# Linear attention on one core: the store of group 9 moved from GpSimd's software queue to SyncE's hardware queue

## The chip, the cores and the metric

One core of one Trainium2 chip. The metric is device time in microseconds (us) of one execution, median of several runs. Some programs have a second, slower state of execution. The profiled span (first to last instruction) is some 1.8 us shorter than the run time of the same execution.

## The reference

```python
# Q, K, V: 8 x 12 x 512 x 64, fp32
Q_feat = np.maximum(0, Q) + 1
K_feat = np.maximum(0, K) + 1
KV = np.einsum('bhkd,bhkv->bhdv', K_feat, V)
K_sum = np.sum(K_feat, axis=2)
numerator = np.einsum('bhqd,bhdv->bhqv', Q_feat, KV)
denominator = np.einsum('bhqd,bhd->bhq', Q_feat, K_sum)
return numerator / (denominator[:, :, :, None] + 1e-10)
```

Three inputs of 12.6 MB are read and one output of 12.6 MB is written: 50.3 MB of HBM traffic.

## The kernel before

The work is cut into 12 groups (NG = 12), each with 1 MB of output. K, V and Q are loaded through GpSimd, and these loads cast from fp32 to bf16 on the way (only the first K comes through SyncE, uncast). Each group's output is stored when its two halves have been normalised on VectorE.

```python
def store(g):
    s = g // 2
    o_to = o_dram[:, 2 * NP * s : 2 * NP * s + 2 * NP]
    if g < NG - 2:                                   # groups 0 to 9: GpSimd
        nc.gpsimd.dma_start(out=o_to[:, g % 2 : 2 * NP : 2], in_=outs[s][:, g % 2 : 2 * NP : 2])
        return
    if g == NG - 2:                                  # group 10: SyncE
        nc.sync.dma_start(out=o_to[:, 0 : 2 * NP : 2], in_=outs[s][:, 0 : 2 * NP : 2])
        return
    for h in range(2):                               # group 11: SyncE, in two halves
        nc.sync.dma_start(
            out=o_to[:, 2 * h + g % 2 : 2 * NP : NP], in_=outs[s][:, 2 * h + g % 2 : 2 * NP : NP]
        )

# ... the loop over groups 0 to 9: loads, compute, store(g - 3); the rest of the compute; store(7) ...
output(last - 1)                # last = 11
output(last)
for g in range(last - LAG, NG): # stores of groups 8, 9, 10, 11
    store(g)
```

(The comments are added here and passages cut, marked by "...". In the traces GpSimd and SyncE each issue their stores in the order of the program, each store after its data: group 9's at 110.19 us, 0.3 us after VectorE's last multiply for it.)

Of the kernel before, what the change touches and what calls it, by code (L numbers as in the profile page):

```python
# [19 lines left out]
def kernel(  # L20
# [19 lines left out]
    nc = tc.nc  # L40
# [8 lines left out]
    NP = 4  # L49
    NG = NPAIR // NP  # L50
# [37 lines left out]
    outs = {}  # L88
# [33 lines left out]
    def store(g):  # L122
        s = g // 2
        o_to = o_dram[:, 2 * NP * s : 2 * NP * s + 2 * NP]
        if g < NG - 2:
            nc.gpsimd.dma_start(out=o_to[:, g % 2 : 2 * NP : 2], in_=outs[s][:, g % 2 : 2 * NP : 2])  # L126
            return
        if g == NG - 2:
            nc.sync.dma_start(out=o_to[:, 0 : 2 * NP : 2], in_=outs[s][:, 0 : 2 * NP : 2])
            return  # L130
        for h in range(2):
            nc.sync.dma_start(
                out=o_to[:, 2 * h + g % 2 : 2 * NP : NP], in_=outs[s][:, 2 * h + g % 2 : 2 * NP : NP]
            )
# [112 lines left out]
    with tc.manual_schedule():  # L247
# [17 lines left out]
        for g in range(last - 1):  # L265
            if g % 2:
                transposes(g - 1)
            k_features(g)
            v_blocks(g)
            if g >= 2:  # L270
                output(g - 2)
            if g % 2:
                transposes(g)
            else:
                q_features(g)
                q_features(g + 1)
            keys_values(g)
            if g % 2 and g // 2 + 2 < NG // 2:
                load_pair(g // 2 + 2)
            if g >= LAG:  # L280
                store(g - LAG)
# [5 lines left out]
        v_blocks(last)  # L287
        keys_values(last - 1)
        store(last - 1 - LAG)
        q_features(last - 1)  # L290
        q_features(last)
# [8 lines left out]
        for g in range(last - LAG, NG):  # L300
            store(g)
# [30 lines left out]
```

## Time and profile before

| | before |
|---|---|
| median time, 3 runs | 126.77 us |
| profiled span | 125.0 us |
| busiest compute engine, VectorE | 89.1 us, 71% |
| DMA engines, share of software queue + hardware queue | 97.2% + 6.7% |

The profile's slice rows cut the span into 40 equal slices of 3.1 us; a digit is the busy share in tenths, and the GB/s row is what the 16 DMA engines moved. The prediction below shows these rows and the tail's timeline. A store has landed when its transfer is complete; the page's "us to landing" is the time from the start of the issuing instruction to the last of the 16 semaphore increments of the transfer.

### The profile page before, as it was taken

What the parts mean: (1) busy time and instruction counts of PE and PEld (TensorE: products, weight loads), DVE (VectorE), ACT (ScalarE), POOL (GpSimd) and SP (SyncE); (2) the same over time, 40 slices, a digit from 0 to 9 for tenths busy, and PEclk for the clock granted to TensorE, in tenths of its full rate; (3) what the DMA queues carried; (4) which work ended last, traced back from release to release, by engine and by line L of the source; (5) the groups of instructions that cost most, each with busy time, mean ns of one, the idle gap of its engine ahead of it and who ended that gap; (6) DMA issues with size and microseconds to landing.
All of it is one profiled execution on the core that took longest, in us unless ns stands there. A gap on an engine that the chain in (4) does not pass through costs nothing.

```text
span 125.0 us, 2348 instructions
## 1 busy us (share of the span) xinstructions
PE 62.7 (50%) x960; PEld 51.3 (41%) x960; DVE 89.1 (71%) x190; ACT 59.6 (48%) x86; POOL 26.1 (21%) x52
## 2 busy tenths in 40 slices
PE   0004945200593837539684691079494457775300
PEld 0003735200482827428573491057393255663100
DVE  4895444206999899997999930799948699969700
ACT  7532289306029781956539462601992295450000
POOL 6991023000001630233302430302020200020000
PEclk9999999955589999995999679756999558997555
DMA  3999999999999999999999999999999999999992
GB/s 94 329 220 207 208 195 208 209 213 214 210 210 212 219 214 207 211 214 220 227 404 328 213 212 214 215 347 391 228 211 216 216 267 417 420 410 417 408 403 103
DMA packets 11803, 32.13 MB, mean 257 GB/s; under 512 B 528, under 2 KB 528, under 8 KB 11792
## 3 DMA queue, kind: packets, MB, share of 16 engines
q0 software_dynamic: 10448, 28.84, 97.2%
q1 hardware_dynamic: 1344, 3.15, 6.7%
q8 instruction: 7, 0.11, 0.3%
q14 instruction: 4, 0.03, 0.1%
HBM read 37.75 MB, written 12.58 MB: 403 GB/s over the span
## 4 chain that ended last, share of the span: by engine, by line
DMA 53%; DVE 23%; PE 8%; ACT 6%; issue 3%; POOL 2%; POOLq 0%
DMA v_raw<-in_V_dram 53%; DVE v_all L155 8%; DVE o_sb L223 8%; PE kva_ps L171 5%; ACT v_all L153 3%; DVE qf L137 2%; PE qt_ps L192 2%; DVE recip L222 2%; ACT qt L195 2%; DVE kf L137 1%; DVE qt L195 1%; ACT kva_all L181 1%; POOL v_raw L106 1%; POOL k_raw L106 1%; PE o_ps L205 1%
## 5 line engine op out<-in xcount | busy, mean ns | idle before, releaser
L205 PE MATMUL o_ps<-kva_all,qt 128*64 128x130 bf16 x384 | 20.5, 244 | 36.9 <-DVE recip L222 27.3
L171 PE MATMUL kva_ps<-v_all,kf 128*64 128x260 bf16 x384 | 30.1, 322 | 15.5 <-DVE v_all L155 15.3
L155 DVE COPY v_all<-v_raw 32x2048 bf16<-32x2048 bf16 x36 | 25.8, 717 | 13.5 <-DMA v_raw<-in_V_dram 13.1
L223 DVE TENSOR_TENSOR o_sb<-o_ps,recip 128x512 f32<-128x512 f32 x48 | 33.2, 692 | 1.7
L171 PEld LDWEIGHTS <-kf 128*64 128x64 bf16 x384 | 24.7, 131 | 18.8 <-DVE v_all L155 15.7
L205 PEld LDWEIGHTS <-qt 128*64 128x64 bf16 x384 | 14.3, 120 | 42.1 <-issue 27.3
L153 ACT COPY v_all<-v_raw 32x2048 bf16<-32x2048 bf16 x12 | 22.6, 1893 | 17.1 <-DMA v_raw<-in_V_dram 16.9
L195 ACT COPY qt<-qt_ps 128x1024 bf16<-128x1024 bf16 x23 | 22.2, 1015 | 6.7 <-PE qt_ps L192 6.4
L181 ACT CAST kva_all<-kva_ps 64x256 bf16<-64x256 f32 x24 | 8.9, 371 | 27.7 <-PE kva_ps L171 27.5
L126 POOL DMA_DIRECT2D out_dram<-o_sb x10 | 8.6, 863 | 35.9 <-DVE o_sb L223 27.5
L192 PE MATMUL qt_ps<-identity,qf 128*128 128x128 bf16 x192 | 14.9, 236 | 1.8 <-ACT qt L195 1.2
L192 PEld LDWEIGHTS <-qf 128*128 128x128 bf16 x192 | 12.5, 106 | 4.5 <-issue 2.5
L137 DVE TENSOR_SCALAR kf<-k_raw 128x1024 bf16<-128x1024 bf16 x22 | 8.5, 429 | 7.8 <-DMA k_raw<-in_K_dram 7.8
L106 POOL DMA_DIRECT2D k_raw<-in_K_dram x6 | 4.9, 811 | 35.2 <-DVE kf L137 35.2
L222 DVE RECIPROCAL recip<-o_ps 128x8 f32<-128x8 f32 x48 | 9.6, 200 | 1.4 <-PE o_ps L205 1.2
L137 DVE TENSOR_SCALAR qf<-q_raw 128x1024 bf16<-128x1024 bf16 x24 | 8.8, 432 | 2.1 <-DMA q_raw<-in_Q_dram 2.1
L106 POOL DMA_DIRECT2D v_raw<-in_V_dram x7 | 5.4, 766 | 13.1 <-ACT v_all L153 9.3
L240 DVE MEMSET v_all<- 128x2600 f32 x2 | 4.5, 2225 | 1.1 <-issue 1.1
L112 POOL DMA_DIRECT2D q_raw<-in_Q_dram x6 | 4.2, 708 | 0.0
L182 ACT CAST kva_all<-kva_ps 64x4 bf16<-64x4 f32 x24 | 4.1, 169 | 0.0
L241 ACT COPY v_all<-zero 128x1560 f32<-128x1560 f32 x2 | 2.9, 1488 | 0.0
L261 POOL MEMSET kva_all<- 128x130 bf16 x16 | 2.4, 201 | 0.0
(13 smaller groups left out, 5.7 us busy)
## 6 DMA issues: line engine op xcount, KB each, us to landing
out_dram<-o_sb POOLq DMA_DIRECT2D x10, 1024.0 KB, 25.9
q_raw<-in_Q_dram POOLq DMA_DIRECT2D x6, 1024.0 KB, 26.2
k_raw<-in_K_dram POOLq DMA_DIRECT2D x5, 1024.0 KB, 21.9
v_raw<-in_V_dram POOLq DMA_DIRECT2D x5, 1024.0 KB, 23.2
k_first<-in_K_dram SPq DMA_DIRECT2D x1, 1024.0 KB, 4.8
v_raw<-in_V_dram POOLq DMA_DIRECT2D x2, 512.0 KB, 10.7
out_dram<-o_sb SPq DMA_DIRECT2D x1, 1024.0 KB, 7.0
out_dram<-o_sb SPq DMA_DIRECT2D x2, 512.0 KB, 6.4
```

What stands on the lines that cost most here:

```text
L106: nc.gpsimd.dma_start(out=bufs[x, s][:, ms], in_=drams[x][:, of])
L126: nc.gpsimd.dma_start(out=o_to[:, g % 2 : 2 * NP : 2], in_=outs[s][:, g % 2 : 2 * NP : 2])
L137: nc.vector.tensor_scalar(out=dst, in0=src, scalar1=1.0, scalar2=1.0, op0=ALU.add, op1=ALU.max)
L153: nc.scalar.copy(out=v_all[ps, g % 2, :, :, b * D : b * D + D], in_=v_raw[ps])
L155: nc.vector.tensor_copy(out=v_all[ps, g % 2, :, :, b * D : b * D + D], in_=v_raw[ps])
L171: nc.tensor.matmul(kva_ps[64 * n : 64 * n + 64], lhsT=kf[:, c, n, :], rhs=v_all[:, g % 2, n, c, :], start=(c == 0), stop=(c == C2 - 1),)
L181: nc.scalar.copy(out=kva[ps, :, n, 0:D], in_=kva_ps[ps, 0 : 4 * D].rearrange("p (b d) -> p b d", b=4))
L192: nc.tensor.transpose(qt_ps[:, c, r], qf[:, r, 2 * half + c, :, :], identity)
L195: copy(out=qts[g // 2][:, lo : lo + 2], in_=qt_ps.rearrange("p c r q -> p c q r"))
L205: nc.tensor.matmul(ops[c // 4][64 * j : 64 * j + 64, c // 2 % 2, (c % 2) * W : (c % 2) * W + W], lhsT=qt[:, c, q : q + 16, :], rhs=kva[:, ...
L222: nc.vector.reciprocal(out=recip, in_=cells[:, :, :, :, D:D1])
L223: nc.vector.tensor_tensor(out=o_sb[:, 2 * h + g % 2 : 2 * NP : NP, 4 * i : 4 * i + 4].rearrange("p n (b c) d -> p b c n d", b=2), in0=cell ...
```

## The change

Intent: take one more of the late stores off GpSimd, which needs 0.75 us to issue it, and give it to SyncE, which needs 0.38 us and is idle until 114.54 us.

```diff
-        if g < NG - 2:
+        if g < NG - 3:
             nc.gpsimd.dma_start(out=o_to[:, g % 2 : 2 * NP : 2], in_=outs[s][:, g % 2 : 2 * NP : 2])
             return
-        if g == NG - 2:
-            nc.sync.dma_start(out=o_to[:, 0 : 2 * NP : 2], in_=outs[s][:, 0 : 2 * NP : 2])
+        if g < NG - 1:
+            nc.sync.dma_start(out=o_to[:, g % 2 : 2 * NP : 2], in_=outs[s][:, g % 2 : 2 * NP : 2])
             return
```

Groups 9 and 10 now go through SyncE; nothing else moves.

## The prediction

> **What bounds the kernel now.** I read the overall page first (busy shares, slices, queues), then the DMA view cut to windows of the tail, the timeline of GpSimd, SyncE and VectorE there, and the landing of each store, and last the waits of SyncE. The page's slices and queues come first:
>
> ```profile
> DVE  4895444206999899997999930799948699969700
> ...
> DMA  3999999999999999999999999999999999999992
> GB/s 94 329 220 207 208 195 208 209 213 214 210 210 212 219 214 207 211 214 220 227 404 328 213 212 214 215 347 391 228 211 216 216 267 417 420 410 417 408 403 103
> ...
> q0 software_dynamic: 10448, 28.84, 97.2%
> q1 hardware_dynamic: 1344, 3.15, 6.7%
> ...
> HBM read 37.75 MB, written 12.58 MB: 403 GB/s over the span
> ```
>
> The DMA row is full from the second slice to the last but one, while VectorE, the busiest compute engine, has gaps and stops two slices (some 6 us) before the end. GB/s is near 210 while loads dominate (they read fp32 and write bf16, so half the bytes that HBM gives are counted) and near 415 once only stores are left, from about 103 us. The 16 DMA engines are the bound, and what counts is bytes per engine. The chain of waits (DMA 53%) ends at the last VectorE multiply at 117.9 us and does not follow the stores after it, so the end has to be read elsewhere.
>
> The tail, from the timeline (columns: start, duration, engine, line, operation):
>
> ```profile
> 98.50 0.75 POOL L126 DMA_DIRECT2D out_dram<-o_sb  x1 [5.24 <-DVE o_sb L223]
> ...
> 110.19 0.75 POOL L126 DMA_DIRECT2D out_dram<-o_sb  x1 [10.94 <-DVE o_sb L223]
> ...
> 111.06 0.21 DVE L222 RECIPROCAL recip<-o_ps 128x8 f32<-128x8 f32 x1 [1.16 <-PE o_ps L205]
> ...
> 114.54 0.38 SPq L129 DMA_DIRECT2D out_dram<-o_sb  x1
> 116.22 2.05 SPq L132 DMA_DIRECT2D out_dram<-o_sb  x2
> ```
>
> These are the issues of the stores of groups 8 and 9 (GpSimd), 10 and the two halves of 11 (SyncE; the second half at 117.90). Adding each one's "us to landing" (21.5 for group 7, issued at 92.50, then 18.0, 9.1, 7.0, 6.6, 6.2) gives the landings: group 7 at 114.0, 8 at 116.5, 9 at 119.3, 10 at 121.5, 11 at 122.8 and 124.1. A 1 MB store that takes 2.5 us from its predecessor's landing to its own was issued up to 21.5 us before: they stand in line. When group 9's store is issued at 110.2, groups 7 and 8 are still in the DMA engines' queues.
>
> Who is served in the tail, from the DMA view in three windows, 112 to 116, 116.5 to 118.5 and 118.5 to 121.5 us (packets, MB, share of the 16 engines):
>
> ```profile
> DMA packets 431, 1.66 MB, mean 416 GB/s; under 512 B 26, under 2 KB 26, under 8 KB 430
> q0 software_dynamic: 430, 1.65, 102.2%
> ...
> DMA packets 315, 0.80 MB, mean 402 GB/s; under 512 B 14, under 2 KB 14, under 8 KB 315
> q1 hardware_dynamic: 209, 0.43, 54.9%
> q0 software_dynamic: 106, 0.38, 46.5%
> ...
> DMA packets 624, 1.23 MB, mean 410 GB/s; under 512 B 24, under 2 KB 24, under 8 KB 624
> q1 hardware_dynamic: 622, 1.23, 105.3%
> ```
>
> The software queue alone moves 416 GB/s in packets of 4 KB, the hardware queue alone 410 in packets of 2 KB, both together 402. None of the three windows has idle engines. From 121.5 us on the engines run dry one after another (0.44 MB in the last 2.2 us).
>
> **What the Trainium skill says.** "DMA: Bandwidth & Descriptors", section "Issuing engines are not separate DMA queues": DMAs issued by different engines run on the same 16 DMA engines, and changing the issuer saves only the sequencer's time. The trace agrees: 416, 410 and 402 GB/s, whoever issues. The same page, "Queues, rings and completion order", says that each DMA engine goes round robin between queues, packet by packet. The trace shows this at most in part: the store of group 10 was issued by 114.92, yet the first packet of the hardware queue starts only at 116.50, after the software queue's work in front was nearly used up on the earliest engine. Its section "SWDGE vs HWDGE vs iDMA" says that descriptors written by GpSimd can be held off by VectorE's two-port modes and that the hardware queue is immune. Here the GpSimd issue at 110.19 took 0.75 us, as short as every undisturbed one, and falls in a stretch where VectorE waits for TensorE (1.16 us before 111.06), so nothing is held off. "Perfetto Trace Analysis", "Summary: the profiler window per engine type", says an issue's recorded time excludes the movement of the data; 0.75 us against 9.1 us to landing agrees.
>
> **The change part by part.**
> Removed: one GpSimd issue, 0.75 us, at 110.19, some 0.3 us after its data were ready (VectorE's multiply ended at 109.20 + 0.69 = 109.89). GpSimd has nothing after it. It holds up no engine: worth 0 us. In the software queue, 256 packets of 4 KB go.
> Added: one SyncE issue of 0.38 us, at about 109.9. SyncE is idle until the store of group 10 at 114.54, so that store and group 11's keep their times; 0 us. In the hardware queue, 512 packets of 2 KB are added (1 MB).
> Bytes per DMA engine: unchanged. At the two queues' own rates 1.05 MB costs 1.05/0.410 - 1.05/0.416 = 2.56 - 2.52 = +0.04 us.
> Moved: store 9 may start about 0.3 + 0.4 = 0.7 us earlier. It does not help, because groups 7 and 8 lie before it or beside it, and every engine is full from 103 to 121.5 us. What store 9 gains, store 8 loses: I expect store 8 to land between 116.5 and 120, and store 9 between 117 and 119.5. Group 10 and the halves of 11 stand behind it in the one queue, with the same total in front of them, so they should land where they do now.
> Mixing: both queues would now be active together for perhaps 5 to 8 us in place of 2. At 402 against 413 GB/s (mean of both alone) each us of mixing costs 11/413 = 0.027 us; 5 us more is +0.13 us. That 402 may be chance in so short a window, so I take half: +0.07.
> Compute: o_sb has three buffers, and the buffer that group 9 fills is never written again, so nobody waits for a landing. VectorE and TensorE keep their times.
> Sum: 0 + 0 + 0.04 + 0.07 = +0.1 us on 126.77. Predicted 126.9 us, unchanged for all practical purposes.
>
> **The rivals.**
> 1. The issue path matters: if the earlier start (0.7 us) and the shorter issue (0.75 against 0.38) came through to the end, the time would be about 125.8. Against it stands the full DMA row: an earlier place in a line of fixed length does not shorten the line.
> 2. The tail evens out. The last 0.44 MB take 2.2 us because the engines end at different times; evenly spread at 413 GB/s they need 1.07. If the hardware queue evened the engines, up to 1.1 us would go: 125.7. Against it: both queues split a store over all 16 engines alike, and the packets carry the same bytes per engine, so the lag of the slowest engine should stay.
> 3. SyncE blocks. 3 MB then go through one hardware queue where 2 MB did. If its descriptor space were full, the issues of groups 10 and 11 would wait. Waiting costs nothing while data are in front, but if the last half were issued only when the store before the previous one had landed, the engines would have gaps; two gaps of about 1.3 us (one half's time) make 129.4. For: this depth is not seen in the trace. Against: at 117.90 the last half was issued in 0.37 us with about 1.3 MB of group 10 and the first half of group 11 still in that queue, and after the change the queue should hold at most about 1 MB more than that.
> 4. Group 8, left in the software queue, is starved and lands last, after group 11. Total work is the same, so the time too, but the last landing would be another store's.
>
> **Range and chances.** The runs before spread over 126.35 to 126.81, or 0.36%. The known terms are within 0.2 us of zero; rivals 1 and 2 reach 0.9% faster, rival 3 alone reaches 2% slower (129.4 is 2.1%). I give them 10% together as partial effects, and so take 126.3 to 127.3 as the range. Faster by over 2% would need 2.5 us, more than the whole uneven tail can return: 0.01. Slower by over 2%: 0.02, from rival 3. Within 2%: 0.97.
>
> **What would show each step right or wrong.** In the changed profile the hardware queue should hold about 4.2 MB (3.15 + 1.05) and the software queue 1.05 MB less than 28.84; the GpSimd store count should be 9. The store of group 9 should appear on SyncE near 109.9 for about 0.38 us, and groups 10 and 11 near 114.5, 116.2 and 117.9 (rival 3: later or longer issues). The DMA row should stay full, 400 to 417 GB/s, up to about 121.5 us, and the last landing should lie within 0.3 us of 124.1, still the second half of group 11 (rival 4: another store). The tail after 121.5 should hold about 0.44 MB (rival 2: less, and a sharper end). The prediction is wrong if a slice between 110 and 121 us drops under 390 GB/s, or if the end moves by more than 0.5 us.

## The result and the profile after

Median 126.70 us over 6 runs (126.49 to 126.87), against 126.66 over 6 runs of the kernel before (126.35 to 127.01). The ratio is 1.0003, 95% interval 0.9982 to 1.0025: no change. (Ratios here and below are the mean time of one kernel's fast runs over that of the other's fast runs of the same rounds, so not quite the ratio of the medians quoted.)

The page of the changed kernel, its DMA slices and its two queues:

```profile
DMA  4999999999999999999999999999999999999992
GB/s 84 333 220 206 212 192 209 210 217 214 207 213 212 218 214 207 212 212 219 227 412 326 210 210 217 218 342 392 227 212 216 216 265 419 421 412 412 405 404 108
...
q0 software_dynamic: 10176, 27.79, 95.0%
q1 hardware_dynamic: 1872, 4.19, 9.1%
```

1.05 MB have moved from the software queue (28.84 MB before) to the hardware queue (3.15 before). The DMA row is as full as it was, and the last seven slices carry the same GB/s within 5.

The timeline of the changed kernel's tail (start, duration, engine, line, operation):

```profile
109.90 4.99 SPq L129 DMA_DIRECT2D out_dram<-o_sb  x2
...
111.03 0.21 DVE L222 RECIPROCAL recip<-o_ps 128x8 f32<-128x8 f32 x1 [1.16 <-PE o_ps L205]
...
116.19 2.06 SPq L132 DMA_DIRECT2D out_dram<-o_sb  x2
```

The row "109.90 4.99 ... x2" merges the issues of groups 9 and 10 with the wait between them; each issue by itself took 0.38 and 0.37 us. VectorE waits for TensorE at 111.03 exactly as before (1.16 us), so compute has not noticed the change. Landings, each worked out as issue start plus time to landing:

| store of group | before: issued, landed | after: issued, landed |
|---|---|---|
| 8 | 98.50, 116.5 | 98.47, 117.8 |
| 9 | 110.19, 119.3 | 109.90, 119.0 |
| 10 | 114.54, 121.5 | 114.51, 121.5 |
| 11, first half | 116.22, 122.8 | 116.19, 122.8 |
| 11, second half | 117.90, 124.1 | 117.87, 124.1 |

Group 9 lands 0.3 us earlier and group 8 1.2 us later: group 9's packets now take turns with group 8's. Everything behind them lands when it did.

The DMA view of the window 112 to 116 us of the changed kernel (in the kernel before, this window had the software queue alone, 416 GB/s):

```profile
DMA packets 537, 1.64 MB, mean 410 GB/s; under 512 B 19, under 2 KB 19, under 8 KB 536
...
q0 software_dynamic: 299, 1.15, 70.7%
q1 hardware_dynamic: 237, 0.49, 31.4%
```

Both queues share the engines from 113.5 us on, three us earlier than before (116.5). The mean of this window includes 1.5 us of the software queue alone: from 113.5 to 116 us the two together moved 406 GB/s, where the software queue alone had moved 413 in the kernel before.

### The profile page after: what moved, and what is told of

Read it like the earlier page. It is cut to its first block, busy times and chain, and to the rows that moved or that the text cites. A ratio compares the mean times of both kernels' runs of the same rounds, so it can differ in the third digit from the quotient of the medians.

```text
span 125.0 us, 2347 instructions
## 1 busy us (share of the span) xinstructions
PE 65.6 (52%) x960; PEld 53.5 (43%) x960; DVE 89.5 (72%) x190; ACT 59.6 (48%) x86; POOL 25.3 (20%) x51
## 4 chain that ended last, share of the span: by engine, by line
DMA 51%; DVE 23%; PE 9%; ACT 6%; issue 3%; POOL 2%; POOLq 0%
DMA v_raw<-in_V_dram 51%; DVE v_all L155 9%; DVE o_sb L223 8%; PE kva_ps L171 7%; ACT v_all L153 3%; DVE qf L137 2%; DVE recip L222 2%; ACT qt L195 2%; PE qt_ps L192 1%; DVE kf L137 1%; DVE qt L195 1%; ACT kva_all L181 1%; POOL v_raw L106 1%; POOL k_raw L106 1%; PE o_ps L205 1%
## 5 line engine op out<-in xcount | busy, mean ns | idle before, releaser
L171 PE MATMUL kva_ps<-v_all,kf 128*64 128x260 bf16 x384 | 34.5, 354 | 15.7 <-DVE v_all L155 15.2
L205 PE MATMUL o_ps<-kva_all,qt 128*64 128x130 bf16 x384 | 19.6, 236 | 34.5 <-DVE recip L222 26.5
L171 PEld LDWEIGHTS <-kf 128*64 128x64 bf16 x384 | 28.1, 145 | 19.7 <-DVE v_all L155 15.6
L205 PEld LDWEIGHTS <-qt 128*64 128x64 bf16 x384 | 13.7, 116 | 39.5 <-issue 22.7
L192 PE MATMUL qt_ps<-identity,qf 128*128 128x128 bf16 x192 | 14.3, 231 | 1.1 <-ACT qt L195 0.8
L192 PEld LDWEIGHTS <-qf 128*128 128x128 bf16 x192 | 12.0, 104 | 3.9 <-issue 2.0
L126 POOL DMA_DIRECT2D out_dram<-o_sb x9 | 7.7, 860 | 22.7 <-DVE o_sb L223 16.4
L106 POOL DMA_DIRECT2D v_raw<-in_V_dram x7 | 5.4, 765 | 15.4 <-ACT v_all L153 11.6
```

The costliest lines, as they stand in the source:

```text
L106: nc.gpsimd.dma_start(out=bufs[x, s][:, ms], in_=drams[x][:, of])
L171: nc.tensor.matmul(kva_ps[64 * n : 64 * n + 64], lhsT=kf[:, c, n, :], rhs=v_all[:, g % 2, n, c, :], start=(c == 0), stop=(c == C2 - 1),)
L192: nc.tensor.transpose(qt_ps[:, c, r], qf[:, r, 2 * half + c, :, :], identity)
L205: nc.tensor.matmul(ops[c // 4][64 * j : 64 * j + 64, c // 2 % 2, (c % 2) * W : (c % 2) * W + W], lhsT=qt[:, c, q : q + 16, :], rhs=kva[:, ...
```

## The experiments

Theory: from the start to 121.5 us the 16 DMA engines have work waiting, so the end is set by the bytes in line ("the line" below is all that waits for these engines, in either queue); the queue that a late store stands in does not matter. Rivals: the path of issue and landing of the stores sets the end; the hardware queue fills up and blocks SyncE; the queue shapes the uneven tail. A further possibility is that the choice of queue matters and two effects cancelled in this change. All runs of experiments were on one chip, each kernel beside the kernel before (median there 126.61 to 126.69 us). "Landing" is that of the last store in the profile, and each kernel has one profiled execution.

| kernel | median us | ratio to before, 95% interval | last landing | span |
|---|---|---|---|---|
| before | 126.66 | | 124.07 | 125.0 |
| changed | 126.70 | 1.0003 (0.9982 to 1.0025) | 124.08 | 125.0 |
| group 9 issued last | 126.93 | 1.003 (1.001 to 1.005) | 124.39 | 125.3 |
| group 9 left out | 124.13 | 0.9808 (0.979 to 0.9826) | 121.89 | 122.8 |
| all stores on GpSimd | 128.14 | 1.011 (1.0087 to 1.0132) | 123.65 | 125.8 |
| only the last half on GpSimd | 127.70 | 1.0084 (1.0071 to 1.0097) | 123.89 | 125.9 |
| groups 6 to 9 left out, rest SyncE | 124.16 | 0.9808 (0.9781 to 0.9834) | 121.17 | 122.5 |
| groups 6 to 9 left out, rest GpSimd | 125.59 | 0.9912 (0.9896 to 0.9928) | 121.93 | 123.9 |
| groups 8 to 11 on SyncE | 126.96 | 1.0026 (1.0011 to 1.0041) | 124.53 | 125.4 |
| groups 7 to 11 on SyncE | 128.06 | 1.012 (1.0045 to 1.0195) | 125.14 | 126.1 |
| groups 6 to 11 on SyncE | 131.84 | 1.0408 (1.0382 to 1.0434) | 129.76 | 131.1 |

### Group 9 issued last

```diff
-        for g in range(last - LAG, NG):
+        for g in (last - 3, last - 1, last, last - 2):
             store(g)
```

> The changed kernel, with the store of group 9 issued on SyncE after all other stores: at about 118.3 us in place of 109.9, 8.4 us later. Theory (the 16 DMA engines have a full line, so the end is set by bytes alone): 126.7 us within 0.4; groups 10 and 11 land about 2.5 us earlier than now (119.0, 120.3, 121.6) and group 9 lands last, at about 124.1. Rival (the issue-to-landing path of each store sets the end): group 9 lands 9.1 us after its issue, at 127.4, and the time is about 130.

Measured: 126.93 us, 0.3% slower than before. The store of group 9 was issued at 118.55 (8.7 us later than in the changed kernel) and landed last, at 124.39. The rival would have had it land 9.1 us after its issue, at 127.7; it took 5.8 us. So it is no surprise that ending its issue 0.7 us earlier, as the change does, is worth nothing that can be measured. The theory held in size, but not fully: the page of this run shows the line running short once, for want of group 9's bytes:

```profile
DMA  3999999999999999999999999999999999998994
GB/s 99 330 213 210 210 181 212 211 214 219 206 211 211 218 216 206 213 212 218 233 412 313 203 211 218 214 344 393 228 210 215 222 269 415 420 415 326 407 408 170
```

By an estimate from these rows, the slice with 326 GB/s (415 before it) lacks 0.28 MB, or 0.7 us of the line, and the fuller last slice (170 against 103) gives back 0.5 us; that is about the 0.3 us that the end moved. How early a store is issued matters only down to the point where nothing else is in line.

### Group 9 left out

```diff
-        for g in range(last - LAG, NG):
+        for g in (last - 3, last - 1, last):
             store(g)
```

> The changed kernel without the store of group 9 (its rows are wrong on purpose). Theory: 1.05 MB less in the line, at about 0.415 MB per us, so 2.5 us less: 124.2 us, within 0.4; the last landing (second half of group 11) at about 121.6. Rival (the path of compute and issue of the last half sets the end, and group 9 is hidden): no change, 126.7.

Measured: 124.13 us, 2.5 us less than before (rows of group 9 wrong). Issue times of the other stores did not move earlier (the last half was issued at 118.2, 0.3 us later), and the last landing came 2.2 us earlier, at 121.89. This refutes the rival that compute and issue of the last half set the end of the kernels before and after. But the landing moved less than the 2.5 us that its bytes are worth, because the line now ran short (324 GB/s, before the store of group 10 came):

```profile
DMA  3999999999999999999999999999999999999894
GB/s 79 332 217 212 204 198 208 213 211 220 207 212 212 214 218 206 214 212 214 216 344 402 216 210 213 216 236 416 322 208 213 214 217 324 423 419 414 324 408 172
```

Here compute already has a part in setting the end: leaving out three stores more gives the same time (124.16 us, below). That the time fell by just the 2.5 us of the bytes is in part luck.

### All stores on GpSimd

```diff
-        if g < NG - 3:
+        if g < NG - 1:
             nc.gpsimd.dma_start(...)
             return
-        if g < NG - 1:
-            nc.sync.dma_start(...)
-            return
         for h in range(2):
-            nc.sync.dma_start(
+            nc.gpsimd.dma_start(
```

> All twelve stores through GpSimd's software queue, also groups 10 and 11. Theory: 126.7 us within 0.4, the last half issued some 0.7 us later (0.3 us of wake-up and 0.75 against 0.37 us of issue) but landing at about 124.1 all the same. Rival issue path: +0.7 us, 127.4. Rival uneven tail: if the hardware queue shapes the tail after 121.5 us, its 0.44 to 0.48 MB and 2.2 us change, and the time with them, by up to 1 us.

Measured: 128.14 us, 1.1% slower; a miss for the theory as it was stated. Yet the last landing was not later: 123.65 against 124.07. The time was lost after it. SyncE's waits in this kernel (who waited for what: us in total, times, longest):

```profile
SPq L324 <- DMA out_dram<-o_sb: 122.3, 5, 115.0
SPq L324 <- PEq L324: 1.8, 2, 1.3
```

In the changed kernel the same two waits of the kernel's closing lines read:

```profile
SPq L327 <- DMA out_dram<-o_sb: 5.4, 4, 2.5
...
SPq L327 <- PEq L327: 0.7, 2, 0.5
```

The closing wait of SyncE for the other engines has grown from 0.5 to 1.3 us at its longest. The view names TensorE's sequencer; the single instruction records of the trace show that the engine that came late is GpSimd. Its closing DRAIN instruction ends some 1.2 us after the last store that it issued has landed:

```text
kernel                 last GpSimd store landed   GpSimd's DRAIN ended   SyncE's own waits done
before                        119.27                    120.50                 124.16
changed                       117.75                    118.94                 124.18
all stores on GpSimd          123.65                    125.00                 123.80
```

SyncE is ready 0.1 us after the last landing; GpSimd takes 1.35 us. Before the change, GpSimd's drain ended 3.7 us before SyncE's waits, and after it 5.2 us. The change gained slack where there already was slack. This profiled execution was the fastest of six (127.52 us, span 125.8); the other five had spans from 125.9 to 126.7, so the rest of the 1.5 us in the median is not seen in this profile.

### Only the last half on GpSimd

```diff
         for h in range(2):
-            nc.sync.dma_start(
+            (nc.gpsimd if h else nc.sync).dma_start(
```

> The changed kernel with only the very last store (second half of group 11, 0.5 MB) on GpSimd. If the kernel with all stores in software was slow because GpSimd's closing drain ends some 1.3 us after its own last store landed: the same cost here, 127.9 to 128.1 us, the last landing at about 124.1 as now. If it was slow because of the number of bytes in the software queue: 126.7 to 126.9.

Measured: 127.70 us, 0.84% slower than before, with only 0.5 MB moved to the software queue. The last landing is at 123.89, as early as ever; GpSimd's DRAIN ended at 125.12, 1.23 us after it, and SyncE had been done at 124.41 (it waits for this store first and then goes through seven more checks of 0.06 us). SyncE's waits at the end:

```profile
SPq L327 <- DMA out_dram<-o_sb: 7.5, 1, 7.5
...
SPq L327 <- PEq L327: 1.3, 2, 0.8
```

So most of the cost, 1.1 of the 1.5 us, comes from which queue has the very last store. Whether the number of stores in the queue adds the other 0.4 us is not settled: the two intervals (1.0087 to 1.0132 and 1.0071 to 1.0097) overlap. The expected 127.9 to 128.1 was at least 0.2 too high; in the profile the last landing came 0.2 us earlier than in the changed kernel.

### The tail without a line, on SyncE and on GpSimd

Groups 6 to 9 are not stored at all, so that the line is empty when groups 10 and 11 come. One kernel has these on SyncE as the changed kernel does, the other on GpSimd. Their outputs are wrong, which doesn't matter for the times.

```diff
     def store(g):
+        if 6 <= g <= 9:
+            return
         s = g // 2
```

> The changed kernel with the stores of groups 6 to 9 left out (wrong on purpose), so that the DMA engines' line is empty when groups 10 and 11 are stored from SyncE. The end is then set by compute, issue and one transfer. From the stores in the kernel with group 9 left out and with six hardware stores, where a half met an empty line and landed 3.3 to 3.7 us after its issue at about 118: landing at 121.5, time 123.8 us. If the time were the line of bytes alone, it would be 126.7 - 10 = 116.6.

> The same with groups 10 and 11 stored from GpSimd. Here issue and queue lie on the path: issue 0.72 against 0.37 us (+0.35), and GpSimd's last drain, which in the traces so far ended 1.2 to 1.35 us after its last store landed, against SyncE's own wait that ends at the landing: +1.3. So about 125.3 us, 1.5 over the run with the hardware queue; about 124.1 if the drain costs nothing; no difference if the choice of queue never matters.

Measured: 124.16 us on SyncE and 125.59 on GpSimd. The expected 123.8 and 125.3 were each 0.3 to 0.4 too low. First, on SyncE it is no faster than leaving out group 9 alone (124.13), though 3 MB more are gone. (Its last landing is 0.7 us earlier, but its span ends 1.31 us after the landing, against 0.88 there; in its closing records 0.43 us pass between two semaphore instructions of GpSimd where the other takes 0.07. Why is open.) The windows 112 to 116, 116 to 118 and 118 to 121 us of the SyncE kernel (length, then busy time and number of instructions of TensorE, its weight loads, VectorE, ScalarE and GpSimd; then granted clock, DMA share and GB/s):

```profile
112.00:116.00 4.00, 2.09 (x40) 1.30 (x40) 3.83 (x10) 0.00 (x0) 0.00 (x0) 0.97 0.14 54
116.00:118.00 2.00, 0.65 (x8) 0.40 (x8) 1.80 (x5) 0.00 (x0) 0.00 (x0) 0.50 1.05 410
118.00:121.00 3.00, 0.00 (x0) 0.00 (x0) 0.00 (x0) 0.00 (x0) 0.00 (x0) 0.50 0.92 354
```

The DMA engines are nearly idle until the store of group 10 arrives, while VectorE is busy for 3.83 of 4 us. Here compute and issue set the end: the last half is issued at 117.89 and lands at 121.17. In the changed kernel it is issued at 117.87 and lands at 124.08. The line of bytes is therefore 2.9 us longer than the path of compute, issue and one transfer; that is all the slack there is.

Second, with no line the queue counts: GpSimd is 1.43 us slower, about as expected (1.5). The parts were not as expected: the last half lands 0.76 us later (121.93) in place of 0.35, and the span ends 1.95 us after the landing against 1.31, so 0.64 us more in place of 1.3. GpSimd's DRAIN ends at 123.12, 1.19 us after the landing as elsewhere, but the SyncE kernel's own slow end hides a part of it. That the sum fits is in part luck. The change moved a store that is neither last nor without a line in front of it, so neither part applied.

### More stores on SyncE

Three kernels, with the stores from group 8, 7 and 6 on through SyncE:

```diff
-        if g < NG - 3:
+        if g < NG - 4:    # from group 8;  NG - 5: from group 7;  NG - 6: from group 6
```

> Stores of groups 6 to 11 on SyncE's hardware queue, 0 to 5 on GpSimd. Theory: 126.7 us within 0.6, whether or not the early ones (issued from about 84 us, while loads are in the line) pass the loads. Rival (the hardware queue fills up and holds SyncE): issues much longer than 0.38 us, the later stores issued late, gaps in the DMA row, 129 us or more. If the hardware queue is served in turn with the software queue, packet by packet, stores 6 and 7 land within about 5 to 8 us of issue and the loads land some us later; if it stands behind it, they land some 20 to 27 us after issue, as now.

> Stores of groups 8 to 11 on SyncE. The store of group 8 is issued at 98.5, when one load (q of the last pair, landing at 103.9) is still in the line. The hardware queue's first packet came 3.5 us after its issue twice behind a full line, so at 102: it passes only the last part of that load and otherwise only stores. Expected: the load lands at most 1 us later, compute moves by less, no gap in the DMA row, 126.7 us within 0.4. If the six-store version was slow because of the number of stores in the hardware queue, in proportion: about 1.3 us slower, 128.

> Stores of groups 7 to 11 on SyncE. If the cost of six hardware stores comes from stores that pass loads, here one store more passes them than in the version from group 8: issued at about 92.5, served from about 96 (3.5 us later, as seen three times), before v and q of the last pair have landed (99.1 and 103.9 now). One store is 2.5 us of the engines' time, and the store of group 8 may pass q as well: v lands 1 to 2.5 us later, q 2.5 to 4, the last half is issued 1 to 3 us later than 117.9 with about 2.9 us of slack there, so 127 to 129 us, between the version from group 8 (126.96) and from group 6 (131.84). If passing loads is harmless: 126.7 to 127.0. All stores of the tail then still show full 16 engines unless compute moves past the slack.

Measured: 126.96, 128.06 and 131.84 us from group 8, 7 and 6. SyncE was never blocked: its issues took 0.37 or 0.38 us in all three (once, in the kernel with group 9 issued last, 0.51). So the rival of a full queue falls, up to these six groups. In the kernel from group 6 the stores of groups 6 and 7 landed 13.1 and 15.4 us after their issue, between the two forecasts (5 to 8 and 20 to 27). What happens instead is in the page of the kernel from group 6:

```profile
DMA  4999999999999999999999999999999999948194
GB/s 92 322 216 206 215 201 207 214 219 207 212 212 215 216 208 212 212 217 222 402 322 189 212 214 219 371 354 262 267 266 267 259 251 366 419 169 316 66 407 176
```

From about 88 us on, GB/s is at some 262 in place of 212: loads and stores move side by side. Some 25 us later the line runs empty (169, 66 GB/s). The DMA view of its window 90 to 100 us:

```profile
DMA packets 1326, 2.66 MB, mean 266 GB/s; under 512 B 32, under 2 KB 32, under 8 KB 1325
...
q0 software_dynamic: 661, 1.32, 69.6%
q1 hardware_dynamic: 664, 1.33, 39.3%
```

The queues take turns packet by packet, 661 to 664. The stores pass loads that were issued 15 us before them. VectorE in the kernel from group 6, and then in the kernel before (what it waits for is in brackets):

```profile
105.53 2.08 DVE L155 COPY v_all<-v_raw 32x2048 bf16<-32x2048 bf16 x3 [3.50 <-DMA v_raw<-in_V_dram]
...
111.85 1.43 DVE L137 TENSOR_SCALAR qf<-q_raw 128x1024 bf16<-128x1024 bf16 x4 [1.46 <-DMA q_raw<-in_Q_dram]
```

```profile
99.10 2.08 DVE L155 COPY v_all<-v_raw 32x2048 bf16<-32x2048 bf16 x3 [0.90 <-DMA v_raw<-in_V_dram]
...
103.97 1.43 DVE L137 TENSOR_SCALAR qf<-q_raw 128x1024 bf16<-128x1024 bf16 x4
```

(The operations shown are those that use the last V and the last Q.) The last V comes 6.4 us later and the last Q 7.9 us later. The last half is then issued at 126.50 in place of 117.90; that eats the slack of 2.9 us and leaves the rest as idle DMA engines. The three kernels make a series: the last Q lands 0.9, 3.0 and 7.9 us later than before (104.88, 106.92, 111.83 against 103.95), the last half is issued 0.9, 4.0 and 8.6 us later, and the median moves by 0.35, 1.4 and 5.2 us (126.96, 128.06, 131.84 less the 126.61, 126.69, 126.61 beside them). Within the slack of 2.9 us a late issue is nearly free; what goes beyond it, 1.1 and 5.7 us, shows as about that much time. The kernel from group 8 came out as expected. For the kernel from group 7 the issue was expected 1 to 3 us later and was 4.0; the time was in the expected range. The expectation for the kernel from group 6 that the theory holds "whether or not the early ones pass the loads" was wrong.

Stores do not pass at once. Behind a long line of software stores or loads the first packet of the hardware queue started 3.2 to 3.7 us after the issue began (six cases: 85.71 to 89.22 in the kernel from group 6, 92.47 to 95.96 from group 7, 98.50 to 102.00 and 110.85 to 114.03 from group 8, 109.90 to 113.49 in the changed kernel, and 109.74 to 113.40 with only the last half on GpSimd), and 0.91 or 0.92 us after it when the line was empty (117.80 to 118.71 and 123.15 to 124.06 in the kernel from group 6, 114.53 to 115.45 without groups 6 to 9). In the kernel before it was 2.0 us (114.54 to 116.50): there the software queue had only some 2 us of work left on the earliest engine. The store of group 9 is issued at 109.9, 6 us after the last load has landed (103.92), so it has no load to pass: by this account it is safe to move.

No experiment points to a version that beats both kernels: the line of bytes is the same in all correct ones, and every other order of queues tried was equal or slower.

## Why the prediction was right

The mechanism was right, and not only the number. Two effects that cancel are not seen: the last landing (124.07 and 124.08) and the time from it to the end of the span (0.89 and 0.91 us) are each unchanged.

- **The bound.** The full line of the DMA engines sets the end: shown by leaving out group 9, which brought the last landing 2.2 us forward with nothing issued earlier. What the prediction did not know is how thin this bound is. Compute, issue and one transfer would end only 2.9 us sooner by themselves.
- **Removed (GpSimd's issue, worth 0).** Right for the time. But the step said that GpSimd "has nothing after it", and that was not so: its closing DRAIN follows, and ends 1.2 us after the landing of its last store. It had 3.7 us to spare for group 9; for the last store of the kernel the same cost shows in full (0.84% with the last half alone).
- **Added (SyncE's issue).** At 109.90, for 0.38 us; groups 10 and 11 kept their times. As predicted.
- **Moved (an earlier start is worth nothing).** As predicted, group 8 lost and group 9 gained, both inside the predicted stretches (117.8 and 119.0), though the loss (1.2 us) was larger than the gain (0.3). The prediction named groups 7 and 8 as still in line at 110.2 us; group 6 was too (it landed at 111.5). Shown from the other side: issuing group 9 8.7 us later costs 0.3 us.
- **Mixing (+0.07) and slower packets (+0.04).** The queues were active together for 3.8 us (113.5 to 117.3), where the prediction had 5 to 8, because the first packet of store 9 came 3.6 us after its issue. From 113.5 to 116 us they moved 406 GB/s together, against 413 for the software queue alone in the same stretch before: the loss by mixing is nearer to 2% than to the 3% that 402 suggested, and both are single windows. The measured difference of medians is 0.04 us with an interval of some 0.3 us to either side; these terms are too small to be confirmed or refuted.
- **Rival 1, the issue path.** Refuted for this store. It is real where the line is empty: of the 1.43 us between the two kernels without groups 6 to 9, the later landing is 0.76.
- **Rival 2, the tail evens out.** It did not: 0.48 MB after 121.5 us, against 0.44. It evened out only where the line broke (with group 9 issued last, for one), and there the gap cost more than the even end gave. With all stores on GpSimd the 16 increments of the last store still spread over 1.74 us, against 2.06 before.
- **Rival 3, SyncE blocks.** Not seen with up to six stores on SyncE. The danger on this side is another one, which the prediction did not list: stores that pass loads.
- **Rival 4, group 8 starves.** It did not: group 8 landed at 117.8, still before group 9.
- **Round robin.** The prediction read the late start of the hardware queue as a sign that queues do not really take turns. The run from group 6 corrects this: they do, packet for packet, once the hardware queue has begun, 3.2 to 3.7 us after the issue in a long line. The result did not hang on this reading.

What stays open: why the hardware queue begins so late behind a full line; why one of the 16 engines ends 2 us after another in the kernels with an unbroken line; and 0.7 us of the cost of all stores on GpSimd, which its profiled execution did not have.

## What to carry to other kernels

In this kernel the DMA row is full to the end, and moving a late store to another queue changed who lands first and not when the last lands. To test whether another kernel is like this, leave out one transfer and see whether the end moves by its bytes; if it moves by less, or if leaving out more does not help, compute is close behind. The choice of queue counted here in three places: for the last store (an empty line, or GpSimd's closing drain), for a store that can pass loads on which compute waits, and where nothing stands in front of it. Before moving more, measure the slack between the line of bytes and the path of compute: here it was 2.9 us, and two more stores moved the same way used it up.

## What the Trainium skill lacked or had wrong

- "DMA: Bandwidth & Descriptors", section "Issuing engines are not separate DMA queues", says that the choice of issuing engine saves only sequencer time. The total rate agrees (410 against 416 GB/s), but the choice also decides the place in line: the stores of six groups on SyncE cost 4.1%, because they passed loads in the software queue.
- The same page, "Queues, rings and completion order", gives the turn by packets, and the runs agree (661 to 664 packets). It lacks that the hardware queue's first packet came 3.2 to 3.7 us after the start of the issue behind a long line in the software queue (six cases; 0.91 or 0.92 us in an empty one, three cases).
- No page that was read says that GpSimd's closing drain ends 1.1 to 1.35 us after the landing of its last software-queue store, while SyncE is done 0.1 us after the landing of its own: 0.84% when only the last 0.5 MB were stored from GpSimd.
